# Three staging tiles in turn for the later output-weight blocks of a hybrid attention and mLSTM layer

## The chip, the cores and the metric

The kernel runs on one core of one Trainium2 chip. The metric is the device time of one execution in microseconds (us); smaller is better. Five engines run beside each other, each with its own in-order stream of instructions: PE (matrix multiplication; its weight loads are listed as PEld), DVE (vector), ACT (activation and copies), POOL (general elementwise work) and SP, which here issues all DMA transfers. An instruction that has to wait holds everything behind it on its engine.

## The reference

One layer on 1024 latent tokens and 256 context tokens of width 1024, in fp32. A normalised and modulated input goes through one projection into two groups of heads: windowed attention (8 query heads, 2 key/value heads, window 128, all context keys and a sink) and a bidirectional chunkwise mLSTM (4 heads). Their outputs are concatenated and multiplied by the output weight; a SwiGLU sub-layer follows. Cut to what matters here:

```python
att_x = window_attention(qx_att, kx_att, avx, kc_att, vc_att, attn_sink[layer])
ml_x = mlstm_output(h_ml_x, mox, g_mlstm_out[layer])
mix_x = jnp.concatenate([att_x, ml_x], axis=-1) @ w_out[layer]
x = x + gt_m * rms_norm(mix_x, g_post_mix[layer])
fx = swiglu(modulate(rms_norm(x, g_pre_ffn[layer]), sh_f, sc_f), w_ffn_in[layer], w_ffn_out[layer])
x = x + gt_f * rms_norm(fx, g_post_ffn[layer])
```

The output weight is 1024 x 1024. The kernel keeps it as eight blocks of 128 x 1024.

## The kernel before, in words

Large products are formed from split operands: a value is cut into a high part in the reduced format fp32r (a cast on ACT) and a low part (raw minus high), and `mm3` multiplies high by high, high by low and low by high. `split` (L62) does this with ACT and DVE.

**The stages.** The input projection comes first (to about 290 us of the span), then the attention with the mLSTM values beside it (about 290 to 444 us), then the output projection with the residual, and from about 560 us the SwiGLU sub-layer. From L1094 on the order of the instructions is written by hand (`manual_schedule`). Before that point a planner sets it: it simulates the program as it is written and orders each engine's instructions by when their inputs should be there. `issue_after` and `keep_in_program_order` hold single instructions back: the first lets the requests of a block come no earlier in the queue than a given instruction, the second keeps an instruction from being planned ahead of what stands before it in the program.

**The attention loop** (L1052) runs over 16 items, item i being one block of 128 queries (n = i // 2) and one key/value group (g = i % 2). `Soft` (L952) makes scores, exponentials and normalised probabilities of item i + 2; its buffer `pr` is normalised in place by POOL (L988). `Values` (L990) transposes the probabilities on PE (`tr`, L1002), splits them (`th` on ACT, `tl` on DVE, L64 and L65), multiplies by the values (`mm`, L1012 and L1013) and combines the result (`out`, L1020 on ACT and L1021 on DVE; "O" in the plan). The strings `PLAN_ML`, `PLAN` and `PLAN13` give the order in which an item's steps are written down. Items 0 to 7 also carry the mLSTM of chunk i (`ml_load`, `ml_scores`, `ml_values`, `ml_norm`, `ml_out`); items 8 to 13 do not. The last two items are written by hand, mixed with the first products of the output projection (`omm`, tiles `op`).

**The output weight.** The eight raw blocks are fetched and split while the attention runs. The table says which item splits which block:

```python
WR = ((1, 2), (4, 5), (6, 7), (0, 3), (14, 15), (10, 13), (12, 8), (9, 11))
WTRIP = (3, 6, 7)
WLOADS = {8: (3, 6), 9: (7,)}
WSPLIT = {1: 3, 2: 6, 3: 7, 5: 0, 6: 4, 7: 1, 8: 2, 9: 5}
```

At the start of item i, `wout_raw(i)` (L916) requests block `WSPLIT[i]` into the one staging tile `wor` (L924, request L926, 512 KB). Step "p" near the end of the item, `wout_split(i)` (L931), makes the high part on ACT (L938) and the low part on POOL (L939). Both are kept in program order. The blocks 3, 6 and 7 (`WTRIP`, items 1 to 3) have no resting place yet, so their parts go to the tiles `woxh` and `woxl`, are stored to DRAM by `wout_raw` of the next item (L921) and come back with `wout_load` in items 8 and 9 (L945). The blocks 0, 4, 1, 2 and 5 (items 5 to 9) are split straight into their final tiles (`woh`, `wol`). So `wor` is used eight times in a row, each request waiting for the subtraction L939 of the split before, and `woxh` and `woxl` are not used after item 4's stores.

**The SP queue** in this stretch carries, beside L921, L926 and L945, the query loads `q_load(i + 3)` (L724, four transfers of an item), and for items with mLSTM work the weights (L838), queries (L850) and output gates (L852) of the next chunk. The list `qlast` holds the newest query load; the raw request is held behind it by `issue_after(qlast[0])`.

Of the kernel before, what the change touches and what calls it, by code (L numbers as in the profile page):

```python
# [9 lines left out]
F32 = mybir.dt.float32  # L10
# [6 lines left out]
P = 128  # L17
D = 1024
# [22 lines left out]
WSPLIT = {1: 3, 2: 6, 3: 7, 5: 0, 6: 4, 7: 1, 8: 2, 9: 5}  # L41


def body(tc, x, ctx, vecs, bcv, bada, gqm, gqf, wada, ws1, ws2, wt, wout, wfi, wfo,
# [3 lines left out]
    dma = nc.sync.dma_start  # L48
# [667 lines left out]
    qhl, prs, wo, qlast = {}, {}, {}, [None]  # L716
# [23 lines left out]
    for j, name in enumerate(TILES):  # L740
# [5 lines left out]
        i = int(name[-1]) if name[-1].isdigit() else 0  # L746
# [55 lines left out]
        if 0 <= j - 3 < 9:  # L802
            s_ = j - 3
            if s_ >= 1 and s_ % 2 == 1:
                k = (s_ - 1) // 2
# [14 lines left out]
    qa = atp[1]  # L820
# [93 lines left out]
    wraw = {}  # L914

    def wout_raw(i):  # L916

        j = WSPLIT.get(i - 1)
        if j in WTRIP:
            for d, t in zip(wo_d, wraw.pop(j)):  # L920
                dma(d[j], t.bitcast(F32))  # L921
        if i in WSPLIT:
            j = WSPLIT[i]
            wraw[j] = qa.tile([P, D], F32, name=f"wor{j}", tag="wor", bufs=1)  # L924
            with tc.issue_after(qlast[0]):
                dma(wraw[j], wout[j])  # L926

    def wout_tiles(j):
        return tuple(R(WR[j][p], f"wo{'hl'[p]}{j}", (D,), F32R) for p in range(2))
# [122 lines left out]
    for i in range(NIT):  # L1052
# [4 lines left out]
        if i == NIT - 2:  # L1057
            break
        wout_raw(i)
        for k in (PLAN_ML if i < NT else PLAN13 if i == NIT - 3 else PLAN).split():  # L1060
            op, n = k[0], int(k[1:] or 0)
# [664 lines left out]
    for p in range(4, HT):  # L1726
        j = p - 5
# [265 lines left out]
```

## Time and profile before

| what | us |
|---|---|
| median of 3 runs | 1188.93 |
| lowest, highest | 1188.78, 1191.32 |
| profiled execution | 1189.32 |
| its span, first to last instruction | 1187.5 |
| granted clock of the matrix engine, mean | 0.998 |
| busy in the span: PE, DVE, ACT, POOL | 1164.6, 818.3, 578.1, 152.8 |
| median landing of a raw block's request (8 requests) | 6.2 |

A row of a timeline gives the start from the span's beginning, the duration, engine, line, operation, output and inputs, shape and, in brackets, how long the engine had been idle and what ended that. Requests on SP are listed with the time of issuing; the transfer itself lands later. Tile names carry a number where there are many (`th__4450` is the high part of one transposed probability tile).

### The profile page before, as it was taken

The page shows a single profiled execution, that of the slowest core. Times are in us where ns is not written, and L with a number is a line of the kernel's source. Part 1 is how long each engine was busy: PE and PEld are TensorE (multiplying, and loading weights), DVE is VectorE, ACT ScalarE, POOL GpSimd, SP SyncE. Part 2 cuts the span into 40 slices and gives each one's busy share as a digit, 9 for nine tenths or more (in the row PEclk, how much of TensorE's full clock was granted, in tenths as well). Part 3 has the DMA queues.
Part 4 walks back from the last instruction along what each step waited for, and adds up shares of the span by engine and source line. Part 5 has one row for each costly group of instructions (what it writes and reads, how often), then busy time and mean ns, then how long its engine had stood idle before and what let it go on. Part 6 is the DMA issues. An engine that isn't in the chain of part 4 may idle for free.

```text
span 1187.5 us, 16397 instructions
## 1 busy us (share of the span) xinstructions
PE 1164.6 (98%) x5881; PEld 964.5 (81%) x5881; DVE 818.3 (69%) x1437; ACT 578.1 (49%) x1075; POOL 152.8 (13%) x204
## 2 busy tenths in 40 slices
PE   9899999999999989999999999999999999999997
PEld 3799888877888877888788888888888888888886
DVE  5864768863989984468767767776777656544566
ACT  6743442222877885777533334333333335434543
POOL 1550001225544550000000000000000000000000
PEclk9999999999999999999999999999999999999999
DMA  9522955648886713321242675656553557665853
GB/s 367 196 72 64 376 191 168 186 132 245 207 223 162 220 38 99 150 91 52 87 142 97 218 241 200 216 202 221 204 182 123 191 186 269 201 220 181 310 186 124
DMA packets 101992, 214.89 MB, mean 181 GB/s; under 512 B 10004, under 2 KB 39316, under 8 KB 100504
## 3 DMA queue, kind: packets, MB, share of 16 engines
q1 hardware_dynamic: 101912, 213.85, 54.4%
q8 instruction: 46, 0.75, 0.3%
q14 instruction: 34, 0.28, 0.1%
HBM read 157.19 MB, written 55.97 MB: 179 GB/s over the span
## 4 chain that ended last, share of the span: by engine, by line
PE 82%; DVE 10%; DMA 3%; ACT 2%; issue 2%; POOL 1%; SPq 0%; DVEq 0%; ACTq 0%; POOLq 0%
PE xv L78 8%; PE xv L76 8%; PE xv L77 8%; PE pt L78 6%; PE pt L76 6%; PE pt L77 6%; PE t L596 3%; PE t L595 2%; PE t L598 2%; PE op L78 2%; PE op L76 2%; PE op L77 2%; PE fx L76 2%; PE fx L78 2%; PE fx L77 2%
## 5 line engine op out<-in xcount | busy, mean ns | idle before, releaser
L65 DVE TENSOR_TENSOR fo<-fr,fo 128x1024 fp32r<-128x1024 f32 x77 | 92.7, 1222 | 70.9 <-ACT fo L64 70.6
L64 ACT CAST fo<-fr 128x1024 fp32r<-128x1024 f32 x77 | 79.7, 1052 | 73.9 <-PE pt L78 33.2
L595 PE MATMUL t<-hh,th 128*128 128x512 f32 x208 | 82.4, 396 | 0.0
L596 PE MATMUL t<-hl,th 128*128 128x512 f32 x208 | 81.7, 393 | 0.0
L1399 ACT CAST wS<-wr 128x512 fp32r<-128x512 f32 x88 | 54.2, 623 | 55.2 <-PE pt L78 36.6
L1401 DVE TENSOR_TENSOR wS<-wr,wS 128x512 fp32r<-128x512 f32 x88 | 60.4, 688 | 19.8 <-ACT wS L1399 19.7
L76 PE MATMUL xv<-tT,wS 128*128 128x512 f32 x168 | 65.6, 391 | 0.0
L78 PE MATMUL xv<-tT,wS 128*128 128x512 f32 x168 | 65.6, 391 | 0.0
L598 PE MATMUL t<-hh,tl 128*128 128x512 f32 x208 | 65.6, 393 | 0.0
L77 PE MATMUL xv<-tT,wS 128*128 128x512 f32 x168 | 65.5, 390 | 0.0
L76 PE MATMUL op<-woh,mh 128*128 128x512 f32 x128 | 51.0, 398 | 0.0
L77 PE MATMUL op<-wol,mh 128*128 128x512 f32 x128 | 50.0, 391 | 0.0
L78 PE MATMUL op<-woh,ml 128*128 128x512 f32 x128 | 50.0, 390 | 0.0
L1147 DVE TENSOR_TENSOR wr<-wr 128x512 f32<-128x512 f32 x66 | 45.5, 690 | 1.4
L1433 ACT ACTIVATE es<-es 128x512 f32<-128x512 f32 x22 | 13.9, 632 | 66.5 <-DVE es L1150 66.5
L595 PEld LDWEIGHTS t<-hh,th 128*128 128x128 f32 x208 | 39.1, 188 | 8.3 <-issue 0.3
L596 PEld LDWEIGHTS t<-hl,th 128*128 128x128 f32 x208 | 39.1, 188 | 7.8 <-issue 0.8
L598 PEld LDWEIGHTS t<-hh,tl 128*128 128x128 f32 x208 | 37.4, 188 | 6.9 <-issue 0.5
L76 PE MATMUL pt<-fo 128*128 128x512 f32 x110 | 42.8, 389 | 0.0
L77 PE MATMUL pt<-fo 128*128 128x512 f32 x110 | 42.8, 389 | 0.0
L78 PE MATMUL pt<-fo 128*128 128x512 f32 x110 | 42.8, 389 | 0.0
L972 PE MATMUL s<-k,qh 128*128 128x256 f32 (+1 forms) x128 | 40.5, 327 | 0.9 <-DVE sm L974 0.8
(1016 smaller groups left out, 3403.1 us busy)
## 6 DMA issues: line engine op xcount, KB each, us to landing
wr<-in_wfi SPq DMA_DIRECT2D x44, 512.0 KB, 4.8
wb<-in_wada SPq DMA_DIRECT2D x24, 512.0 KB, 5.8
s_d<-a SPq DMA_DIRECT2D x22, 512.0 KB, 6.8
bt<-in_wfo SPq DMA_DIRECT2D x44, 256.0 KB, 4.0
tb_d<-bt SPq DMA_DIRECT2D x11, 1024.0 KB, 3.9
fr<-s_d SPq DMA_DIRECT2D x44, 256.0 KB, 4.4
fr<-tb_d SPq DMA_DIRECT2D x44, 256.0 KB, 4.3
fr<-a_d SPq DMA_DIRECT2D x33, 256.0 KB, 4.5
```

Source lines behind the costliest of these rows:

```text
L64: act.copy(hi, raw)
L65: dve.tensor_tensor(lo, raw, hi.bitcast(F32), SUB)
L76: pe.matmul(ps, a[0], b[0], start=first, stop=False, **kw)
L77: pe.matmul(ps, a[0], b[1], start=False, stop=False, **kw)
L78: pe.matmul(ps, a[1], b[0], start=False, stop=last, **kw)
L595: pe.matmul(o, wh[:, kt], m[0], start=f, stop=False)
L596: pe.matmul(o, wh[:, kt], m[1], start=False, stop=False)
L598: pe.matmul(o, wl[:, kt], m[0], start=False, stop=l)
L972: pe.matmul(o, qh[:, h, :], k2[g][:, kc], start=True, stop=False)
L1147: dve.tensor_tensor(out, a, b, SUB)
L1399: act.copy(w[:, 0], raw)
L1401: dve.tensor_tensor(w[:, 1], raw, w[:, 0].bitcast(F32), SUB)
```

## The change

The raw block of items 5 to 9 is requested one item earlier, at the start of item i - 1, and goes to one of three tiles in turn: block 0 (item 5) to `wor`, block 4 (item 6) to `woxh`, block 1 (item 7) to `woxl`, block 2 (item 8) to `wor`, block 5 (item 9) to `woxh`. Items 1 to 3 are as before. `woxh` and `woxl` keep their size (128 x 1024 values of four bytes), so no memory is added. Copies, subtractions, stores and loads of the other parts of the weight are unchanged, and so are the plans.

```diff
@@ -919,11 +919,12 @@
         if j in WTRIP:
             for d, t in zip(wo_d, wraw.pop(j)):
                 dma(d[j], t.bitcast(F32))
-        if i in WSPLIT:
-            j = WSPLIT[i]
-            wraw[j] = qa.tile([P, D], F32, name=f"wor{j}", tag="wor", bufs=1)
-            with tc.issue_after(qlast[0]):
-                dma(wraw[j], wout[j])
+        for k in [i] if i < 4 else [i + 1]:
+            if k in WSPLIT:
+                j = WSPLIT[k]
+                wraw[j] = qa.tile([P, D], F32, name=f"wor{j}", tag=("wor", "woxh", "woxl")[max(k - 5, 0) % 3], bufs=1)
+                with tc.issue_after(qlast[0]):
+                    dma(wraw[j], wout[j])
```

## The prediction

> **What bounds the kernel now.** I read the page's first part, then the busy time by stretches, then the chain of waits and the timelines of the attention's tail. The page says that the matrix engine is the bound of the whole:
>
> ```profile
> PE 1164.6 (98%) x5881; PEld 964.5 (81%) x5881; DVE 818.3 (69%) x1437; ACT 578.1 (49%) x1075; POOL 152.8 (13%) x204
> ```
>
> So only a stretch in which PE idles can give time back. The columns of the next rows are the stretch, its length, busy time (and instructions) of PE, PEld, DVE, ACT and POOL, the PE clock, the DMA share and GB/s.
>
> ```profile
> 355.00:410.00 55.00, 53.53 (x381) 47.10 (x381) 49.69 (x143) 45.80 (x129) 28.02 (x30) 1.00 0.68 184
> 410.80:430.80 20.00, 16.07 (x105) 13.73 (x103) 16.05 (x36) 15.98 (x33) 12.24 (x13) 1.00 0.46 122
> ```
>
> From 355 to 410 us, where the mLSTM work fills the attention items, PE is busy 53.53 of 55.00. From 410.80 to 430.80, the first items without mLSTM work, PE, DVE and ACT are each busy about 16 of 20 us: all three idle for the same 4 us. The waits of ACT, PE and DVE between 398 and 445 us (total, times, longest) say why:
>
> ```profile
> ACT woh L938 <- DMA wor<-in_wout: 3.9, 2, 2.3
> ```
>
> ```profile
> PE po L1012 <- ACT th__4450 L64: 2.1, 1, 2.1
> PE po L1012 <- ACT th__4560 L64: 1.5, 1, 1.5
> ```
>
> ```profile
> DVE tl__4561 L65 <- ACT th__4560 L64: 1.6, 1, 1.6
> DVE tl__4451 L65 <- ACT th__4450 L64: 1.5, 1, 1.5
> ```
>
> ACT stands twice before the high-part copy of an output-weight split (L938) because the raw block has not landed; the casts th__4450 and th__4560 queue behind that copy on ACT, and PE and DVE wait for them. The ACT timeline has the two copies, with the idle time in brackets:
>
> ```profile
> 415.56 1.04 ACT L938 CAST woh<-wor 128x1024 fp32r<-128x1024 f32 x1 [2.27 <-DMA wor<-in_wout]
> ...
> 424.78 1.04 ACT L938 CAST woh<-wor 128x1024 fp32r<-128x1024 f32 x1 [1.58 <-DMA wor<-in_wout]
> ```
>
> These are the splits of items 8 (block 2) and 9 (block 5), and the view of the instructions of L938 counts no other such wait in the whole span (us, times):
>
> ```profile
>   DMA wor<-in_wout: 3.9, 2
> ```
>
> The chain of waits runs through the second transfer itself:
>
> ```profile
> 420.07 4.69 DMA wor<-in_wout
> ```
>
> Why the transfers are late: the POOL timeline (first fence) gives the low-part subtractions (L939), the last readers of the single staging tile, and the SP timeline (second) the requests.
>
> ```profile
> 383.53 2.41 POOL L939 TENSOR_TENSOR wol<-wor,woh 128x1024 fp32r<-128x1024 f32 x1
> ...
> 396.03 2.41 POOL L939 TENSOR_TENSOR wol<-wor,woh 128x1024 fp32r<-128x1024 f32 x1
> ...
> 407.63 2.40 POOL L939 TENSOR_TENSOR wol<-wor,woh 128x1024 fp32r<-128x1024 f32 x1
> ```
>
> ```profile
> 385.97 0.34 SPq L926 DMA_DIRECT2D wor<-in_wout  x1
> ...
> 398.85 0.56 SPq L926 DMA_DIRECT2D wor<-in_wout  x1
> ...
> 410.17 0.55 SPq L926 DMA_DIRECT2D wor<-in_wout  x1
> ```
>
> The subtractions end at 385.94, 398.44 and 410.03, and each request follows by 0.03 to 0.41 us. The tile, not the queue, holds the request. Block 2's copy begins 5.39 us after its request (415.56 - 410.17). In the items with mLSTM work, which are longer, this is hidden; in the short ones it does not fit.
>
> **The change part by part.** No computing instruction is added or removed: the eight requests, copies and subtractions stay. What moves is five requests and the tiles behind them.
>
> Block 0 (item 5) keeps the tile `wor`, which the subtraction of item 3 frees, so its request stays where it is, at 360.93 in the fence below: gain nothing. Blocks 4 and 1 (items 6 and 7) go to `woxh` and `woxl`, which are free once the parts of block 7 have been stored. Their splits show no wait now, so their earlier landing gains nothing either. But the requests have a new wait: for a store's landing. The SP timeline and the stores' own landing times (least, median, longest):
>
> ```profile
> 358.46 0.55 SPq L921 DMA_DIRECT2D wo_dh<-woxh  x1
> ...
> 360.55 0.33 SPq L921 DMA_DIRECT2D wo_dl<-woxl  x1
> 360.93 0.42 SPq L926 DMA_DIRECT2D wor<-in_wout  x1
> 361.44 1.43 SPq L724 DMA_DIRECT2D qh<-aq_dh  x2
> ```
>
> ```profile
> DMA to landing us min/median/max: 3.2/3.3/5.5
> ```
>
> `woxh` is free at about 361.8 and `woxl` at 363.9 (360.55 + 3.3), at the latest 366.1. Queued behind on SP are the query loads from 361.44 on and the mLSTM loads of the last chunk. Lower bound of this wait's cost: nothing, if the program puts the two requests behind those loads. Upper bound: a block from 361.44 to 366.1, 4.7 us. I take nothing, since the requests of before came 0.03 to 0.41 us after their releases with no waiting engine behind them.
>
> Block 2 (item 8) goes to `wor` again, free after item 5's subtraction at 385.94; block 5 (item 9) to `woxh`, free after item 6's at 398.44. So their requests can go at 386 and 398.5 in place of 410.17 and 420.07, some 24 and 21 us earlier. Even with the page's median landing below, they are there by 392.2 and 404.7, ahead of the copies by over 15 us.
>
> ```profile
> wor<-in_wout SPq DMA_DIRECT2D x8, 512.0 KB, 6.2
> ```
>
> Both DMA waits of ACT disappear: 2.27 + 1.58 = 3.85 us on ACT, 2.1 + 1.5 = 3.6 on PE, 1.5 + 1.6 = 3.1 on DVE. What is late next? The copy itself (1.04 us) and the subtraction (2.40) remain. Each item then runs at the pace of the fullest of three nearly equal engines, for ACT, DVE and PE have 15.98, 16.05 and 16.07 us of work in the same 20. The smallest of the three recoveries, DVE's 3.1 us, is what I take for the stage. Upper bound: ACT's whole idle time, 20.00 - 15.98 = 4.0. Lower bound: DVE reaches only its share of the stretch before, 49.69 / 55.00 = 0.903, so 16.05 / 0.903 = 17.8 and the gain is 2.2.
>
> Does this reach the end? The next stretches, with the same columns:
>
> ```profile
> 444.00:560.00 116.00, 115.71 (x561) 95.74 (x560) 69.48 (x111) 82.68 (x169) 2.73 (x4) 1.00 0.28 100
> 560.00:1187.50 627.50, 621.41 (x2733) 511.95 (x2732) 419.80 (x575) 253.71 (x381) 0.96 (x1) 1.00 0.55 189
> ```
>
> PE is full from 444 us on and the order there is written by hand, so all that follows slides forward as one; no transfer of that part is tied to a fixed time. Sum: -3.1 us with the new SP wait at nothing. The profiled execution took 1189.32 us, 1.82 more than its span of 1187.5; it would take 1186.2. It lay 0.39 above the median of the runs shown, so the median goes from 1188.93 to **1185.8**.
>
> **The rivals.** *The stage paces itself (rival B).* Where ACT does not wait for data, its copies stand right behind their predecessor in the program:
>
> ```profile
> 394.68 0.21 ACT L903 ACTIVATE sq<-sq 128x4 f32<-128x4 f32 x1
> 394.79 1.04 ACT L938 CAST woh<-wor 128x1024 fp32r<-128x1024 f32 x1
> ```
>
> So the copies of items 8 and 9 would move ahead of casts and exponentials that today overtake them, and 1.04 us of copy would lie before work that DVE wants. If each copy leaves a gap of 0.7 us, about two thirds of itself, 3.1 - 1.4 = 1.7 us remain: 1187.2. Against it: DVE has other reductions ready at these points.
>
> *A blocked queue (rival H).* SP issues in order. If block 2's request stood ahead of the last query and mLSTM loads, it would hold them till 385.94. From the timelines of SP and PE, with the landing times of L850 between:
>
> ```profile
> 376.90 0.57 SPq L850 DMA_DIRECT2D qz<-q_dr  x1
> ```
>
> ```profile
> DMA to landing us min/median/max: 2.3/4.7/7.1
> ```
>
> ```profile
> 394.24 0.61 PE L876 MATMUL pt<-cs,qz 128*128 128x129 f32 x4
> ```
>
> Some six issues of 0.57 us go first, so that load would go at 389.4, land at 394.1 (at the latest 396.5), and PE wants it at 394.24: 0 to 2.3 us late. At the longest, 3.1 - 2.3 = 0.8 us remain: 1188.1. Against it: item 6's request waited for the same release at 385.97 and stood behind these loads. The Trainium skill, page "DMA: Bandwidth & Descriptors", section "Anatomy of one DMA — SWDGE (gpsimd) path", says that DMA engines never wait on semaphores; the issuing sequencer does, before it dispatches. By that rule every request with an unfinished release blocks all loads behind it, and this change moves two requests onto a store's landing; the trace agrees in that each request of before left within 0.41 us of its release, but shows no load that came late through it.
>
> *It doesn't do what it says (rival N).* The requests leave no earlier, because the tile release or the order of the queue ties them to something else: 1188.9. Against it: the releases at 385.94 and 398.44.
>
> *Slower (rival S).* The order before 444 us is planned anew from the changed program. A subtraction that goes earlier on POOL stands in front of a normalisation that PE's transposes need. Today (POOL, then PE):
>
> ```profile
> 428.28 1.60 POOL L988 TENSOR_SCALAR pr__4494<-pr__4494,sm 128x640 f32<-128x640 f32 x2
> ```
>
> ```profile
> 433.62 0.60 PE L1002 MATMUL pt<-vec,pr__4494 128*128 128x128 f32 x4
> ```
>
> This half is done at 429.88 and wanted at 433.62, a slack of 3.7 us against 2.40 for a subtraction. It decides once the order eats that slack. If the splits of items 7, 8 and 9 each cost PE 2.40, that is 7.2 - 3.1 = 4.1 us more: 1193.0. Against it is the slack.
>
> **How the numbers follow.** A measurement of this kernel can tell about 0.2%, 2.4 us, from no change. Forecast 0.58 (gain 2.4 to 4.0, 1184.9 to 1186.5), B 0.20 (to 1188.0), H 0.06, N 0.06, S 0.10. Faster by over 0.2% is the forecast, 0.58; B, H and N are within it, 0.32; S 0.10. The range reaches from the upper bound of 4.0 us, with 0.1 for the run, at 1184.8, to 1189.1, which takes in B, H and N and leaves out S.
>
> **What would show it.** Right: five raw loads into three tiles, those of blocks 2 and 5 at about 386 and 398.5; no idle time before L938 in items 8 and 9; PE's waits for the two casts gone; POOL still subtracting for 2.40 us; the output projection's first matmul about 3.1 us earlier, and the same shift at the end. B shows as new gaps of half a microsecond and more on DVE or PE in the 20 us behind O of item 8; H as late mLSTM matmuls between 380 and 400; S as PE waiting for POOL's normalisation. Wrong in general: a different order of the items between 360 and 410, with time lost there, or a shift at 444 us that is not found at the end.

## The result, and the profile after

The changed kernel takes 1186.9 us (median of 10 executions, 1186.39 to 1187.88), the kernel before 1190.37 us on the same chip (10 executions, 1188.78 to 1191.89). The ratio is 0.9974, with a 95% interval of 0.9964 to 0.9983: faster by about a quarter of a per cent. The two profiled executions took 1189.32 and 1186.39 us, 2.93 us apart. That is near the 3.1 us forecast, but two errors cancel in it, as the experiments show.

In absolute terms the median lies 1.1 us above the forecast of 1185.8, within the stated range but in the band that was given to rival B; the difference of 3.5 us lies in the band of the forecast. The two disagree because the forecast started from 1188.93, the median of the three executions known then, and ten gave 1190.37.

The busy times of the whole span, which is now 1184.6 us long, are the same work in less time:

```profile
PE 1165.3 (98%) x5881; PEld 964.7 (81%) x5881; DVE 818.3 (69%) x1437; ACT 579.1 (49%) x1075; POOL 152.5 (13%) x204
```

Did the requests move? The SP timeline of the changed kernel (start, duration, request; lines from L924 on stand one lower than before, so L926 has become L927):

```profile
360.49 1.32 SPq L927 DMA_DIRECT2D wor<-in_wout  x2
361.91 0.58 SPq L724 DMA_DIRECT2D qh<-aq_dh  x1
...
363.85 0.49 SPq L927 DMA_DIRECT2D wor<-in_wout  x1
...
385.53 0.34 SPq L927 DMA_DIRECT2D wor<-in_wout  x1
...
398.42 0.55 SPq L927 DMA_DIRECT2D wor<-in_wout  x1
```

Blocks 0 and 4 go at 360.49, block 1 at 363.85 behind query and mLSTM loads, block 2 at 385.53 and block 5 at 398.42. The view of the high-part copy (L939) now has nothing between the heading for idle time and the next heading:

```profile
its engine sat idle before it (us, times) until:
who waited for it (us, times):
```

The two stretches read before, again with the busy times of PE, PEld, DVE, ACT and POOL, the PE clock, the DMA share and GB/s:

```profile
410.80:430.80 20.00, 18.79 (x115) 15.22 (x114) 18.16 (x42) 18.57 (x39) 14.12 (x17) 1.00 0.27 68
355.00:410.00 55.00, 53.53 (x380) 47.12 (x380) 50.06 (x145) 45.83 (x130) 28.04 (x30) 1.00 0.75 203
```

The items with mLSTM work are as full as they were (PE 53.53 of 55). In the 20 us behind them PE does 18.79 us of work in place of 16.07, so 1.2 us of its idle time is still there. The ACT timeline shows what changed beside the waits:

```profile
410.37 0.58 ACT L1021 COPY o<-po 64x512 f32<-64x512 f32 x1
410.86 1.05 ACT L939 CAST woh<-wor 128x1024 fp32r<-128x1024 f32 x1
...
418.62 0.58 ACT L1021 COPY o<-po 64x512 f32<-64x512 f32 x1
419.23 1.05 ACT L939 CAST woh<-wor 128x1024 fp32r<-128x1024 f32 x1
```

Both copies now stand directly behind O of their items (410.37 for item 8, 418.62 for item 9), in front of the casts that overtook them before. (From here to about 449 us the planner has also put other instructions of PE, DVE, ACT and POOL in another order; before 411 us only SP's order differs.) DVE waits for the first of those casts:

```profile
412.55 0.69 DVE L65 TENSOR_TENSOR tl__4433<-pt,th__4432 128x512 fp32r<-128x512 f32 x1 [0.88 <-ACT th__4432 L64]
```

POOL subtracts as long as before, a little later than the copies (here for item 8):

```profile
412.05 2.40 POOL L940 TENSOR_TENSOR wol<-wor,woh 128x1024 fp32r<-128x1024 f32 x1
```

The first matmul of the output projection (PE timeline) comes 2.87 us earlier than at 444.03:

```profile
441.16 0.48 PE L76 MATMUL op<-woh,mh 128*128 128x512 f32 x1
```

The first load of the next stage (SP timeline) has gone from 450.74 to 447.83, by 2.91, and the span is 2.9 shorter. What was gained before 444 us arrives whole at the end. Yet O of item 8 is itself 0.42 us earlier than the 410.79 of before, and the copy of item 1, at 331.90 in place of 332.32, already was, ahead of any changed request: that part is scatter between two executions. From O of item 8 to the output projection it is 33.24 us before (444.03 - 410.79) and 30.79 after (441.16 - 410.37). The stage gained 2.45 us.

### The profile page after: what moved, and what is told of

It reads as the page before. It is cut to its first block, busy times and chain, and to the rows that moved or that the text cites. A ratio compares the mean times of both kernels' runs of the same rounds, so it can differ in the third digit from the quotient of the medians.

```text
span 1184.6 us, 16387 instructions
## 1 busy us (share of the span) xinstructions
PE 1165.3 (98%) x5881; PEld 964.7 (81%) x5881; DVE 818.3 (69%) x1437; ACT 579.1 (49%) x1075; POOL 152.5 (13%) x204
## 4 chain that ended last, share of the span: by engine, by line
PE 87%; DVE 7%; DMA 2%; ACT 2%; issue 1%; POOL 1%; SPq 0%; DVEq 0%; ACTq 0%; POOLq 0%
PE xv L78 8%; PE xv L77 8%; PE xv L76 8%; PE pt L77 6%; PE pt L76 6%; PE pt L78 6%; PE t L598 4%; PE t L596 4%; PE t L595 4%; PE op L78 2%; PE op L76 2%; PE op L77 2%; PE fx L76 2%; PE fx L78 2%; PE fx L77 2%; PE slab L77 2%
```

## The experiments

In all of them "stage" means the time from O of item 8 on ACT to the first output-projection matmul on PE. Ratios are to the kernel before on the same chip: median 1190.64 (23 executions) beside the first four, 1190.91 (11) beside the others.

**e_tiles: three tiles, requests not earlier in the program.** The change without its second half:

```diff
-        for k in [i] if i < 4 else [i + 1]:
+        for k in [i]:
```

> Three tiles in turn, but each block requested in its own item again. Theory T (the one staging tile held the requests back; the item in which the request is written does not matter): blocks 2 and 5 are still requested near 386 and 398.5 us, both waits of the copy go, 2.4 to 3.9 us less than before (ratio 0.9967 to 0.9980). Rival R1 (the earlier request is what counts): blocks 2 and 5 are requested near 410 and 420, no gain (ratio 1.000).

Measured: 1186.96 us, ratio 0.9969 (0.9958 to 0.9981). The order on ACT and POOL is that of the changed kernel; on SP only block 1's request has another place. The stage takes 30.8 us here too. Blocks 2 and 5 are requested where the changed kernel has them (SP timeline):

```profile
386.06 0.34 SPq L927 DMA_DIRECT2D wor<-in_wout  x1
...
398.95 0.55 SPq L927 DMA_DIRECT2D wor<-in_wout  x1
```

Three tiles alone give the whole effect. The order before 444 us is planned anyway, and the two requests went out as their tiles came free, though they are written an item later.

**e_early: requests one item earlier, one tile.** The other half alone:

```diff
-                ... tag=("wor", "woxh", "woxl")[max(k - 5, 0) % 3], bufs=1)
+                ... tag="wor", bufs=1)
```

> Requests written one item earlier, but the single tile wor for all eight. Theory T: the tile frees at the same times, the order on every engine is that of the kernel before, and the time is that of before (ratio 1.000, within 0.001), with waits of about 2.3 and 1.6 us before the copies of items 8 and 9. Rival R1: some 3 us less.

Measured: 1191.12 us (1187.85 to 1193.43, 12 executions), ratio 1.0002 (0.9991 to 1.0013), with the order of before on every engine. The request still waits for the subtraction that frees the tile. Its profiled execution (1193.43 us) had longer waits than the profile of before, ACT's (total, times, longest) and PE's first:

```profile
ACT woh L939 <- DMA wor<-in_wout: 5.2, 2, 3.6
...
PE po L1013 <- ACT th__4450 L64: 3.5, 1, 3.5
```

It also lost more time than the waits account for. From O of item 8 to that of item 9 it took 12.98 us against 9.59 before, 3.4 more, for a first wait of 3.61 in place of 2.27, 1.3 more. The clock column of the stretches shows where it went:

```profile
420.00:422.00 2.00, 2.00 (x9) 2.00 (x8) 1.37 (x2) 1.87 (x5) 1.25 (x1) 0.50 0.01 4
422.00:424.00 2.00, 2.00 (x9) 1.70 (x8) 1.68 (x6) 0.01 (x1) 0.05 (x1) 0.50 0.21 60
```

PE was busy all through these 4 us, at half its clock, with 9 matmuls in each 2 us. The profile of before has 15 and 18 in the 4 us behind its wait, at full clock:

```profile
418.00:420.00 2.00, 2.00 (x15) 1.79 (x15) 2.00 (x6) 1.93 (x6) 1.08 (x1) 1.00 0.01 4
420.00:422.00 2.00, 2.00 (x18) 2.00 (x17) 1.97 (x6) 1.95 (x5) 1.21 (x2) 1.00 0.78 176
```

**e_late: the change, with the copies put back behind the first casts of the next item.** Requests and tiles are those of the changed kernel:

```diff
-        for k in (... else PLAN).split():
+        for k in (... else PLAN.replace("T2", "T2 q") if i in (9, 10) else PLAN).split():
-            elif op == "p" and i in WSPLIT:
+            elif op == "p" and i in WSPLIT and i not in (8, 9):
                 wout_split(i)
+            elif op == "q":
+                wout_split(i - 1)
```

> The changed kernel, with the splits of items 8 and 9 written behind the third transpose of the next item, so that PE, DVE and POOL have the order of before and ACT differs from it by one exchange; only the DMA waits are gone. Theory T (the gain is the two waits): 2.4 to 3.9 us less than before (ratio 0.9967 to 0.9980). Rival R2 (the gain is the new order that the planner found for items 9 to 12): at most 1 us less than before (ratio 0.999 to 1.000). If the copy in front of th__4432 costs the changed kernel the 0.88 us of idle DVE seen there, this one is some 0.5 us faster than the changed kernel (ratio about 0.997).

Measured: 1185.47 us (1185.24 to 1185.94, 5 executions), ratio 0.9957 (0.9944 to 0.9970). That is 5.2 us less in the median, more than the 2.4 to 3.9 us that was expected of theory T, and rival R2 is out. The order on PE, DVE and POOL is exactly that of the kernel before, and ACT's differs by one exchange: the second copy has gone ahead of one exponential. So this is the old order with the transfer's waits taken out. Its ACT timeline has no idle time ahead of the copies, which come 2.4 and 1.9 us behind O rather than 0.5 and 0.6:

```profile
410.99 0.58 ACT L1021 COPY o<-po 64x512 f32<-64x512 f32 x1
...
413.37 1.06 ACT L939 CAST woh<-wor 128x1024 fp32r<-128x1024 f32 x1
...
418.27 0.58 ACT L1021 COPY o<-po 64x512 f32<-64x512 f32 x1
...
420.17 1.05 ACT L939 CAST woh<-wor 128x1024 fp32r<-128x1024 f32 x1
```

The stretch behind O of item 8, with the columns of before:

```profile
410.80:430.80 20.00, 19.31 (x125) 16.51 (x124) 19.50 (x46) 19.71 (x42) 13.88 (x16) 1.00 0.28 74
```

ACT is busy for 19.71 of 20 us, DVE for 19.50 and PE for 19.31: in these 20 us no wait is left that is worth taking away. The output projection begins at 440.21 (PE timeline):

```profile
440.21 0.48 PE L76 MATMUL op<-woh,mh 128*128 128x512 f32 x1
```

The stage takes 29.22 us: 4.0 less than before's 33.24, 1.6 less than the 30.79 of the changed kernel. This version beats both: none of its executions is as long as the shortest of the changed kernel (1185.94 against 1186.39), nor as the shortest of e_tiles, which ran beside it (1186.67).

**e_b5: block 5 alone goes early, to a tile of its own.** Block 2 keeps its wait:

```diff
+        for k in [i] * (i != 9) + [9] * (i == 8):
...
+                ... tag="woxh" if k == 9 else "wor", bufs=1)
```

> As before, except that block 5 alone is requested one item earlier into woxh. Theory T: the wait of item 9's copy (1.58 us) goes and that of item 8's (2.27 us) stays; 1.0 to 1.6 us less than before (ratio 0.9987 to 0.9992). Rival R2: no proportion to the wait removed; anything between the changed kernel's 0.9974 and 1.000.

Measured: 1190.51 us (1186.94 to 1192.63, 12 executions), ratio 0.9995 (0.9984 to 1.0005). As a time this says nothing: the interval holds 1. The profile says more. The second wait is gone (ACT waits once), and from O of item 9 to the output projection it takes 22.3 us in place of 23.65; from about there on PE, DVE, ACT and POOL have the order of the changed kernel. But the first wait was longer than in the profile of before (waits of ACT and PE):

```profile
ACT woh L939 <- DMA wor<-in_wout: 2.8, 1, 2.8
PE po L1013 <- ACT th__4450 L64: 2.6, 1, 2.6
```

From 420 to 422 us, behind that wait, the clock is again 0.50, and a gain of 1.3 us can't be seen in times that spread over 5.7 us. Neither theory T (1.0 to 1.6 us) nor rival R2 is decided by this run.

**same_1, same_2, same_3: the kernel before, profiled three more times.** No edit. Is the lower clock a matter of the two edited kernels, or does the kernel before have it too?

> The kernel before, profiled again. The two DMA waits of the copies differ from execution to execution. Theory G (the wait costs its own length, and beyond a PE idle time of somewhere between 2.1 and 2.6 us also a time at half the granted clock): from O of item 8 to O of item 9 the stage takes 7.3 us plus the first wait, and 1.4 to 2.1 us more where PE idled 2.6 us or longer. Rival W (only the waits count): 7.3 us plus the first wait in every execution.

> The kernel before, profiled a second time: as same_1, with another pair of waits. Theory G: 7.3 us plus the first wait, plus 1.4 to 2.1 us exactly where PE idled 2.6 us or longer and the granted clock fell. Rival W: no such addition.

> The kernel before, profiled a third time: as same_1, with another pair of waits. Theory G: 7.3 us plus the first wait, plus 1.4 to 2.1 us exactly where PE idled 2.6 us or longer and the granted clock fell. Rival W: no such addition.

Measured: 1192.0, 1191.7 and 1190.82 us, each with the clock at 0.50 for a time behind block 2's wait. In same_1 the copy's wait stands so in the ACT timeline:

```profile
416.31 1.04 ACT L938 CAST woh<-wor 128x1024 fp32r<-128x1024 f32 x1 [2.69 <-DMA wor<-in_wout]
```

The PE timeline of same_1 around it:

```profile
417.89 0.80 PE L1012 MATMUL po<-th__4450,av 128*128 128x512 f32 x1 [2.55 <-ACT th__4450 L64]
418.48 0.52 PE L972 MATMUL s<-k,qh 128*128 128x384 f32 x1
```

After an idle time of 2.55 us the same two matmuls take 0.80 and 0.52 us which in the profile of before, after 2.13 us, took 0.50 and 0.34:

```profile
417.14 0.50 PE L1012 MATMUL po<-th__4450,av 128*128 128x512 f32 x1 [2.13 <-ACT th__4450 L64]
417.48 0.34 PE L972 MATMUL s<-k,qh 128*128 128x384 f32 x1
```

The stretches of same_1 show how long it lasts. The clock is at 0.50 for half of the first row's stretch, for all of the next two and for nine tenths of the last, some 6.8 us in all, of which PE still idles through the first 0.9:

```profile
416.00:418.00 2.00, 0.11 (x1) 0.11 (x1) 0.13 (x1) 1.69 (x3) 0.56 (x1) 0.75 0.10 36
418.00:420.00 2.00, 2.00 (x7) 1.90 (x8) 1.37 (x3) 2.00 (x5) 1.81 (x1) 0.50 0.02 4
420.00:422.00 2.00, 2.00 (x9) 1.70 (x8) 1.83 (x5) 0.44 (x2) 0.00 (x0) 0.50 0.00 0
422.00:424.00 2.00, 2.00 (x10) 1.82 (x9) 1.21 (x4) 1.39 (x3) 1.48 (x2) 0.55 0.73 188
```

All executions that have block 2's wait, side by side. "Over" is the time from O of item 8 to O of item 9, less the 7.28 us that it takes without a wait in the same order (e_late), less ACT's wait:

| profile | ACT's wait | PE idle | O to O | over | lowest clock of a 2 us stretch | time at half clock |
|---|---|---|---|---|---|---|
| before | 2.27 | 2.13 | 9.59 | 0.04 | 1.00 | 0 |
| same_1 | 2.69 | 2.55 | 12.05 | 2.08 | 0.50 | 6.8 |
| e_b5 | 2.78 | 2.65 | 11.51 | 1.45 | 0.50 | 3.4 |
| same_3 | 2.97 | 2.8 | 11.79 | 1.54 | 0.50 | 3.4 |
| same_2 | 3.31 | 3.2 | 12.67 | 2.08 | 0.50 | 6.8 |
| e_early | 3.61 | 3.48 | 12.98 | 2.09 | 0.50 | 6.8 |

Were the longer times only longer waits, "over" would be near nothing in each row, so rival W is out. It is nothing where the clock held and 1.4 to 2.1 us where it fell. It doesn't follow the length of the wait: it follows the time at half clock, 1.45 and 1.54 us for 3.4 us and 2.08 or 2.09 us for 6.8.

The table looks as if an idle time between 2.13 and 2.55 us set off the drop, as theory G has it. The same traces speak against so simple a rule. In five of the ten profiles (e_late, e_b5, e_early, same_1 and same_2) the clock falls once more, for 3.4 us from about 35 us of the span on, where PE has idled for 0.95 us at most. From e_late, first the PE timeline and then the stretches:

```profile
33.97 0.39 PE L378 MATMUL slab<-w1h,hh 128*128 128x272 f32 x1 [0.95 <-ACT hh L252]
```

```profile
34.00:36.00 2.00, 2.00 (x10) 1.70 (x11) 2.00 (x4) 2.00 (x5) 0.00 (x0) 0.80 1.02 401
36.00:38.00 2.00, 2.00 (x11) 2.00 (x11) 2.00 (x6) 1.33 (x4) 0.00 (x0) 0.50 0.53 204
```

The profile of before has the same idle time of 0.95 us at the same matmul, and a clock of 1.00 behind it.

The half-clock times come in steps: 3.4 us or twice that. In the four profiles that have both drops these begin 382.3 us apart (34.7 and 417.0 in same_1), 112 such steps, though O of item 8 lies up to 0.9 us apart in them. So the changes of the clock seem to fall on fixed points 3.4 us apart, and what counts would be how busy PE was between two of these points, not one idle time alone. That the place of the wait counts fits the next two rows, of 3.41 us each: the emptiest such stretch around the wait in before, and the one that ends with the drop in same_1:

```profile
413.74:417.15 3.41, 1.24 (x8) 0.65 (x6) 1.91 (x6) 1.59 (x3) 1.54 (x4) 1.00 0.63 180
```

```profile
413.57:416.98 3.41, 1.73 (x10) 0.98 (x8) 2.29 (x5) 0.72 (x2) 1.58 (x3) 1.00 0.75 217
```

With PE busy for 1.24 us of its stretch before kept its clock, and with 1.73 us same_1 lost it. All this is read from ten traces, and no run tested it; nor was a kernel tried that keeps PE at work through the wait. That "over" comes with the time at half clock is shown by every row of the table and by the longer matmuls; what sets off the drop stays open.

The times without a profile go the same way, but show less: of the 34 executions of the kernel before that stood beside the experiments, 21 had a mean clock of 0.995 or 0.996 and a median of 1191.62 us; 13 had 0.997 to 0.999 and 1189.44 us. The mean clock holds the early drop as well: same_3, with the drop in the stage alone, and e_late, with the early one alone, both have 0.998.

**e_move: blocks 5 and 2 are split in items 6 and 7, which have mLSTM work.** Three tiles, and the short items have no split at all:

```diff
-WSPLIT = {1: 3, 2: 6, 3: 7, 5: 0, 6: 4, 7: 1, 8: 2, 9: 5}
+WSPLIT = {1: (3,), 2: (6,), 3: (7,), 5: (0,), 6: (4, 5), 7: (1, 2)}
+WTAG = {3: "wor", 6: "wor", 7: "wor", 0: "wor", 4: "woxh", 5: "woxl", 1: "wor", 2: "woxh"}
```

> Three tiles, and the splits of blocks 5 and 2 taken out of the short items: block 5 is split in item 6 beside block 4, block 2 in item 7 beside block 1. If copies and subtractions beside the mLSTM work are nearly free, the stage from O of item 8 to the first product of the output projection takes some 1 us less than the 29.2 us of e_late, and the whole about 0.995 of before. If each further split costs these items its 1.04 us of ACT, the time is that of e_late (0.9957) or longer.

Measured: 1186.08 us (1185.48 to 1189.17, 7 executions), ratio 0.9966 (0.9955 to 0.9977), no better than e_late. The stage, with ACT relieved of two copies, takes 28.2 us, another 1.0 less. But item 7 with two splits (O of item 7 to O of item 8) takes 13.07 us, against 12.07 in the changed kernel, and O of item 7 is 0.67 us later than in the changed kernel. The two copies stand in one block on ACT:

```profile
406.13 1.99 ACT L938 CAST woh<-wor 128x1024 fp32r<-128x1024 f32 x2
```

The items with mLSTM work had no room for them; what the short items gain, the long ones lose. Of what was expected the shorter stage came, and the shorter time did not. What ended the extra microsecond in item 7 wasn't followed further.

## Why the prediction was right, and where it was off

**The staging tile, not the queue, held the requests.** Right. Tiles without earlier requests give 0.9969, earlier requests without tiles 1.0002.

**Both waits of ACT go, and SP's new wait costs nothing.** Right. The landings of the eight raw blocks take 5.4 to 8.1 us and are done long before the copies. On the queue, block 4's request stands directly behind block 0's at 360.49, and a query load follows at 361.91, 0.1 us after the pair. Within the pair SP did wait for a store's landing, with the query load behind it (waits of SP from 355 to 400 us):

```profile
SPq L927 <- DMA wo_dh<-woxh: 0.5, 1, 0.5
```

Block 1's request, which needs the later store, was put behind three other loads and had no such wait. So the new wait that the prediction put between nothing and 4.7 us was 0.5 us on SP; nothing shows that it cost time, for PE has no wait for a DMA between 355 and 410 us. The rule of the Trainium skill, page "DMA: Bandwidth & Descriptors", section "Anatomy of one DMA — SWDGE (gpsimd) path", that the issuing sequencer waits rather than the DMA engine, agrees with these 0.5 us.

**The recovery was taken as DVE's 3.1 us.** This term was too small. In the same order of instructions, with the waits gone, the stage gains 33.24 - 29.22 = 4.0 us (e_late): all the idle time of ACT, the upper bound that the prediction worked out. DVE's waits named in the prediction were not all that it lost: in the same 20 us it now does 19.50 us of work in place of 16.05. The three engines wait for one another all along the stage, so idle time of DVE that was put down to other causes went with the transfer too. As it came out, the row to take was that of ACT, which stood at the head of the chain (3.85 us of waits, 4.0 us idle).

**The copies stay where they are.** The forecast took this at nothing, and it was wrong by 1.6 us. Rival B had seen it: a copy that doesn't wait is placed right behind its predecessor, as at 394.79 us before. It named the mechanism and its place; its price of 0.7 us a copy is close to the 0.88 us gap on DVE. Against e_late, O of item 8 to O of item 9 takes 8.25 us in place of 7.28, so 0.97 for the first copy, and the rest of the stage 22.54 in place of 21.94, so 0.6 for the second. Each price includes the new order that the planner found around the copy; e_late puts that back too, and the runs don't part the two. In medians e_late and e_tiles, which has the changed kernel's order on ACT and ran beside e_late, lie 1.5 us apart. The mechanism of rival B came true beside that of the forecast; 4.0 - 1.6 = 2.4 us is the 2.45 us of the stage, and with the 0.42 us that lay between the two executions anyway, the profiled pair differs by 2.9 us. The sum of 3.1 us was close by luck: the one term was 0.9 too small and the other 1.6 too small with the opposite sign, and scatter made up most of the remainder.

**The profile of before stands for the kernel.** The prediction took the profiled execution as typical, 0.39 us above the median of the three runs shown. It was an execution without the clock drop in the stage; the three more profiles all had it. With the wait the change also takes this drop away, which no term of the sum held: the medians differ by 3.5 us where the stage of the profiled pair differs by 2.45. The Trainium skill, page "TensorE: Matmul & The Clock Gate", section "Part 1: The HAM clock gate (the "warmup" mystery)", says that PE falls to half its clock after at least one idle window of about 3.4 us, and advises, in the section "Why this matters for your kernels", against idle gaps of more than about 3 us. Half the clock agrees with the 0.50 of the profiles, and 3.4 us with the steps in which the drops last here. The advice on gaps is too generous here: 2.55 us of idle time came before a drop in the stage, and 0.95 us at most before the one at 35 us. By the page's figure the waits of 2.1 and 1.5 us that the prediction quoted lay well away from any danger; in three of four profiles of the same kernel the first of these waits was 2.55 to 3.2 us long and came with a drop.

**What follows carries the shift to the end.** Right: 2.87 us at the output projection, 2.91 at the next stage's first load, 2.9 in the span.

**The other rivals.** H (a blocked queue) is out: the stretch from 355 to 410 us is as full as before. N is out by the result. S (POOL in front of a normalisation that PE needs) did not come: the subtractions of items 8 and 9 moved earlier, and PE has no wait for POOL in this stage.

## What to carry to other kernels

Where a load waits for its buffer, look for the release that each late request follows: here a request written earlier did nothing (1.0002) and other buffers did everything (0.9969). When a wait goes, price what the freed instruction is put in front of: here two copies of 1.05 us took back 1.6 of 4.0 us, and putting them behind the casts that they had let pass gave it back. Profile the kernel several times before a sum is made from one of its waits: a wait whose length changes from run to run may cost more than its length, and here its own length did not tell when.

## What the runs showed that was not expected

The same wait for the same transfer was 2.27, 2.69, 2.97 and 3.31 us in four profiles of one kernel, and PE's clock stood at 0.50 for 3.4 or 6.8 us after the three longer ones, at a price of 1.5 to 2.1 us each. This fits the spread in the times of all the kernels that kept block 2's wait, from 3.1 us (before, in its first 10 executions) to 5.7 us (e_b5), while the kernels without it that kept the old places of the splits spread over 0.6 to 1.5 us. The seven executions of e_move spread over 3.7 us, though its copies don't wait, because of a single one at 1189.17 us, which stays unexplained. A profile that happens to be without the drop shows nothing of this: before's own had a clock of 1.00 in every stretch of the stage. And a second drop near 35 us, far from any change, came in five of ten profiles, e_late's among them, where PE's longest idle time was 0.95 us.
